# Staging slots at the start of the down-projection, an early query block, and the end of the attention written into the activation tile: one encoder kernel on one core

## The chip, the core and the metric

The kernel is one program on one NeuronCore of a Trainium2 chip. It runs a whole inference step of a two-layer encoder trunk. The metric is the device time in microseconds (us) from the launch to the end; lower is better. TensorE (PE) multiplies matrices, VectorE (DVE), ScalarE (ACT) and GpSimd (POOL) work element by element, and SyncE (SP) issues nearly all of the DMA transfers.

## The reference, cut to what matters

One prompt of 1024 tokens and eight samples of 16 tokens (128 tokens together) go through the same weights; the width is D = 1024, with 16 heads of 64. Layer 0 attends in a sliding window, layer 1 in a band of chunks over keys and values that are projected once, after layer 0.

```
for l in range(2):
    sh_m, sc_m, g_m, sh_f, sc_f, g_f = split(silu(c) @ w_ada[l] + b_ada[l], 6)
    h = x * (1 + sc_m) + sh_m
    o = band_attend(q(h), k, v, ...)          # l == 0: own k, v; l == 1: the shared k_b, v_b
    x = layer_norm(ALPHA * x + (1 + g_m) * (o @ w_o), ln_g[l, 0], ln_b[l, 0])
    h = x * (1 + sc_f) + sh_f
    u = h @ w_up[l]                           # 1024 -> 2 * 2816
    y = conv_b + sum(conv_w[tap] * u[t - 2 + tap] for tap in range(3))
    a, g = split(y, 2)
    x = layer_norm(ALPHA * x + (1 + g_f) * ((gelu(g) * a) @ w_down[l]), ln_g[l, 1], ln_b[l, 1])
    if l == 0:
        k_b, v_b = split((x * (1 + sc_kv) + sh_kv) @ w_kv_b)
```

Everything is float32. The samples attend also to cached keys and values, and the step returns the new keys, values and convolution rows beside the two outputs.

## The kernel before, in words

**Tiles and products.** The tokens are nine tiles of 128: tiles 0 to 7 are the prompt, tile 8 is the samples. Every operand of a large product is split in two: ACT casts the float32 value to a rounded high part (`copy`, line 161 in the profile), and POOL or DVE subtracts that from the value for the low part (`split`, line 172). A product is then three matmuls (low by high, high by low, high by high). `wload` (line 176 issues the DMA) loads a 128x1024 weight into a staging slot from the ring `self.ws`, and splits it into a pair of weight slots (hi, lo) from the ring `self.wring`. A ring hands out its buffers in turn; a load into a buffer waits until what was read from it before has been read.

**Order.** The program is written stage by stage, and a tile scheduler orders each engine's instructions by a simulated clock and by the dependences. On the chip SP, ACT, DVE and POOL each take their own instructions strictly in that order: an instruction that waits holds up all that stands behind it on its engine.

**Attention.** `qload(c)` and `qblock(c, bi)` load and compute the queries of head pair c (eight pairs; three blocks of 384 tokens each, the matmuls of line 291). The loop over `work` has 64 steps i; each issues scores (lines 544 and 547), softmax sums, transposes of the probabilities (lines 572 and 579), and the product with the values (line 594). Tables say at which step something else is issued: `QAT` the next query blocks, `ITEMS` the 16 sample items (eight samples by two halves p of the heads), `OAT` the reload of the finished outputs. A finished half of head pair c below 7 is normalised on POOL, written to a DRAM scratch `oN`, read back by `oload(c)` and split into the activation tile H. Pair 7 is split into H directly. The sample items go through the DRAM scratch `oSD` (eight 128x128 chunks).

**Output projection.** `out_proj` loads eight half-weights `wo` (its line numbers 967 on), then goes through the tiles in the order 8, 0, 1, ... 7: tile 8 first reads `oSD` and splits it; each tile takes two halves of 24 matmuls of 512 columns (`mmX`, line 304), and is then gated, added to the residual and normalised.

**Up- and down-projection.** The up-projection (line 1196) computes 22 blocks j of 128 channels; the convolution's taps (line 1035) and the product of gate and value run on DVE and POOL, and each block's result `act` is written to DRAM (`actD`, line 1083). The down-projection goes through the tiles in three groups of three, (0,1,2), (6,7,8), (3,4,5). In each group `fetch(j)` loads the weight j (`wdn`) by `wload`, reads the three tiles' part of `actD[j]` (line 1258), casts it on ACT and subtracts on DVE (line 1260), and 18 matmuls of 512 columns use it (line 1267). The staging ring for the weights is five slots in layer 0 and four in layer 1:

```
self.ws = Ring(narrow.items + [F[:, 0:1024]] + ([self.hf] if l else [self.lng, self.lnb]))
acts = Ring([... for i in range(12)])        # 12 pairs of 128x384 in X1
```

`narrow` is the two usual slots ws0 and ws1. `lng`, `lnb` are F[10368:12416], which overlaps F[10492:11644], the convolution's last row `y`; `hf` is F[4224:5248], which overlaps F[3876:5046], the last of the up-projection's buffers for u. In the third group the last 4 (layer 0) or 6 (layer 1) of the 22 weights and acts are kept, so that each tile of the group can be ended by itself. During group 0, after j = 8, `ln_gates` (lines 856 and 857) loads the gates and, in layer 1, `ln_rows` loads the rows of the last normalisation.

Of the kernel before, what the change touches and what calls it, by code (L numbers as in the profile page):

```python
# [10 lines left out]
F32 = mybir.dt.float32  # L11
# [27 lines left out]
QAT = {}  # L39
# [5 lines left out]
OAT = {51: (0, 1), 52: (2,), 53: (3,), 54: (4,), 55: (5,), 61: (6,)}  # L45
# [6 lines left out]
class Ring:  # L52
    def __init__(self, items):
        self.items = items
        self.i = 0

    def next(self):
        r = self.items[self.i % len(self.items)]
        self.i += 1
        return r  # L60
# [37 lines left out]
class Trunk:  # L98
    def __init__(self, ctx, tc, I, O):
# [39 lines left out]
        self.oSD = dr.tile([8, 128, 128], F32, name="oSD")  # L139
# [61 lines left out]
    def ada(self, gi, bank, ring=None):  # L201
# [36 lines left out]
        yield  # L238
# [132 lines left out]
    def attention(self, l, wk):  # L371
# [351 lines left out]
        def item_out(x):  # L723
            p, s = x.p, x.s
            t2 = self.bank(tbk.next())
            nc.tensor.transpose(t2[:, 0:128], osm, self.ident)
            if l == 0:
                if s == 0:
                    self.so = ost.next().rearrange("p (j t) -> p j t", t=128)
                so = self.so[:, :, 16 * s : 16 * s + 16]  # L730
            else:
                so = ost.next().rearrange("p (j q) -> p j q", q=16)
            for a in range(2):
                r = slice(64 * a, 64 * a + 64)
# [36 lines left out]
        for bi in range(3):  # L771
            qblock(0, bi, qw[0])
        items = [item(p, s) for p in range(2) for s in range(8)]
        steps = []
        for i, x in enumerate(work):
# [20 lines left out]
            for c in OAT.get(i, ()):  # L796
                oload(c)
        assert not items
# [167 lines left out]
    def out_proj(self, l, xsrc, xdst, aff):  # L966
        nc, I, H = self.nc, self.I, self.H
        wo = I[("wo0", "wo1")[l]]
# [4 lines left out]
        w = [self.wload(wo[i // 4, i % 4], el="ppppvvvv"[i], dst=d) for i, d in enumerate(loc)]  # L973
# [8 lines left out]
        for t in (8, 0, 1, 2, 3, 4, 5, 6, 7):  # L982
            c0 = t * 128
            if t == 8:
                s3 = self.xring.next().rearrange("p (c t) -> p c t", t=128)
                nc.sync.dma_start(s3, self.oSD.rearrange("c p t -> p c t"))
                self.split(s3, H[:, 0, :, c0 : c0 + 128], H[:, 1, :, c0 : c0 + 128], "a", "v")
            x = self.residual(t, xsrc)
            gate = self.gateP if t < 8 else self.gateS
            for hf in range(2):  # L990
                ps = self.bank(mb.next())
                self.mmX(ps, c0, (w0, w1)[hf], 2, 512)
                cs = slice(hf * 512, hf * 512 + 512)
                nc.vector.tensor_mul(self.tmp[:, cs], ps, gate[:, cs])
            nc.vector.scalar_tensor_tensor(x, x, ALPHA, self.tmp, op0=ALU.mult, op1=ALU.add)
            self.norm_tail(t, x, xdst, aff, False, tb, "a", "pv", Ring([self.xr]), hfr, hdst=self.hD)
# [236 lines left out]
    def down(self, l, xsrc, xdst, affs):  # L1233
# [8 lines left out]
        self.ws = Ring(narrow.items + [F[:, 0:1024]] + ([self.hf] if l else [self.lng, self.lnb]))  # L1242
        acts = Ring([(self.X1[:, i * 768 : i * 768 + 384], self.X1[:, i * 768 + 384 : i * 768 + 768]) for i in range(12)])
        ws = self.wslots
        order = [ws[2], ws[3], ws[0], ws[1]]
# [17 lines left out]
        def mm(j, w, a, gi, i):  # L1263
            for hf in range(2):
                ps = self.bank(GB[gi][2 * i + hf])
                for c, (p, q) in enumerate(((1, 0), (0, 1), (0, 0))):
                    nc.tensor.matmul(  # L1267
# [5 lines left out]
                    )  # L1273
# [33 lines left out]
        for gi, g in enumerate(GR):  # L1307
            keep = KEEP[l] if gi == 2 else 0
            for j in range(NFF - keep):
# [308 lines left out]
```

## Time and profile before

| | |
|---|---|
| median of 3 runs | 2878.46 us (2873.03 to 2889.01) |
| the profiled execution's own time | 2869.84 us |
| its span | 2868.1 us |
| mean granted PE clock | 0.979 |
| PE busy | 2719.9 us (95%) |
| DVE, ACT, POOL busy | 63%, 45%, 40% |
| DMA moved | 471.15 MB, mean 164 GB/s |

The stages of the span, by the first and last matmuls of each: opening to 58 us; layer 0's attention to about 380, its output projection to 495, up-projection to 1040, down-projection to 1353; the shared keys and values to 1565; layer 1's attention to 1959, its output projection to 2073, up-projection to 2565, down-projection to 2854. In the rows of the profile a line as "wh<-F" names what is written and what is read (F, X, H, C are the large tiles; wh, wl, xa pairs of hi and lo parts; ws the narrow staging slots). A figure in brackets behind a row is the idle time just before it on its engine, with what ended it.

### The profile page before, as it was taken

To read this page: it belongs to the slowest core of one execution; us is meant where nothing else is said; L and a number is where in the kernel's file an instruction comes from. 1 tells how busy PE (TensorE), PEld (TensorE's weight loads), DVE (VectorE), ACT (ScalarE), POOL (GpSimd) and SP (SyncE) were. 2 spreads that over 40 slices of the span, in tenths; PEclk is the share of its full clock that TensorE was granted. 3 is DMA by queue.
4 is the path that set the end of the run, shared out by engine and by line. 5 is a ranking of instruction groups with operands and counts; after the bars stand their busy time and mean duration, and the time that the engine had idled before them with its cause. 6 is when DMAs were issued, how large, how long until landed. Compare 5 with 4: busy or idle time off the path is not lost.

```text
span 2868.1 us, 47357 instructions
## 1 busy us (share of the span) xinstructions
PE 2719.9 (95%) x17734; PEld 2419.9 (84%) x17734; DVE 1820.3 (63%) x3674; ACT 1293.0 (45%) x2613; POOL 1157.0 (40%) x761
## 2 busy tenths in 40 slices
PE   7999899999999979999998999879999999999997
PEld 5888678889999968887998888757899999997886
DVE  4477777776667763564113667666797788883763
ACT  3476634433334333543225666652454444453442
POOL 2122424444434446655820122232454433447662
PEclk8999899999999989999999999989999999999999
DMA  8655454553444355664875357674432222246552
GB/s 297 213 166 168 135 171 167 188 191 137 142 157 140 124 174 184 228 218 155 287 239 178 108 154 198 166 216 141 167 122 85 70 80 70 70 147 235 206 197 79
DMA packets 221302, 471.15 MB, mean 164 GB/s; under 512 B 39856, under 2 KB 115840, under 8 KB 221072
## 3 DMA queue, kind: packets, MB, share of 16 engines
q1 hardware_dynamic: 221072, 468.13, 50.0%
q8 instruction: 139, 2.28, 0.3%
q14 instruction: 91, 0.75, 0.1%
HBM read 366.74 MB, written 110.74 MB: 166 GB/s over the span
## 4 chain that ended last, share of the span: by engine, by line
PE 79%; DMA 8%; DVE 5%; issue 2%; POOL 2%; ACT 2%; SPq 1%; POOLq 0%; DVEq 0%; ACTq 0%
PE PS L1196 30%; PE PS L1267 18%; PE PS L291 11%; PE PS L304 9%; PE PS L594 2%; PE PS L572 2%; PE PS L218 2%; PE PS L544 1%; PE PS L547 1%; DMA F<-in_wdn_dram 1%; PE PS L920 1%; DVE F L511 1%; POOL H L172 1%; PE PS L713 1%; DMA kH<-X 1%
## 5 line engine op out<-in xcount | busy, mean ns | idle before, releaser
L1196 PE MATMUL PS<-H,wh 128*128 128x256 f32 (+1 forms) x2560 | 395.2, 297 | 0.0
L1196 PEld LDWEIGHTS PS<-H,wh 128*128 128x128 f32 x2560 | 361.3, 191 | 0.4 <-issue 0.4
L1260 DVE TENSOR_TENSOR xa<-xa 128x384 fp32r<-128x384 f32 x132 | 186.7, 1426 | 226.1 <-ACT xa L161 223.9
L172 POOL TENSOR_TENSOR wl<-ws,wh 128x1024 fp32r<-128x1024 f32 x78 | 194.3, 2496 | 300.9 <-ACT wh L161 287.3
L161 ACT CAST wh<-F 128x512 fp32r<-128x512 f32 (+1 forms) x238 | 163.8, 693 | 326.1 <-PE PS L1196 153.1
L1267 PE MATMUL PS<-wh,xa 128*128 128x512 f32 x864 | 277.5, 397 | 25.1 <-ACT wh L161 25.1
L1158 DVE TENSOR_TENSOR F<-PS,F 128x192 f32<-128x192 f32 (+2 forms) x600 | 192.1, 350 | 167.8 <-PE PS L1196 164.9
L291 PE MATMUL PS<-H,wh 128*128 128x384 f32 (+1 forms) x1536 | 294.4, 337 | 0.0
L291 PEld LDWEIGHTS PS<-H,wh 128*128 128x128 f32 x1536 | 266.9, 188 | 1.4 <-issue 1.0
L1035 DVE SCALAR_TENSOR_TENSOR F<-F 128x1024 f32<-128x1024 f32 x320 | 257.6, 845 | 5.8 <-ACT F L1074 4.6
L1196 PE MATMUL PS<-H,wl 128*128 128x256 f32 (+1 forms) x1280 | 229.2, 299 | 9.7 <-ACT F L1163 5.5
L161 ACT CAST wh<-ws 128x1024 fp32r<-128x1024 f32 (+1 forms) x164 | 135.9, 834 | 221.8 <-PE PS L1196 92.2
L172 DVE TENSOR_TENSOR wl<-F,wh 128x512 fp32r<-128x512 f32 x198 | 200.9, 1022 | 37.7 <-ACT wh L161 37.7
L1267 PEld LDWEIGHTS PS<-wh,xa 128*128 128x128 f32 x864 | 163.9, 190 | 66.2 <-ACT wh L161 26.0
L1196 PEld LDWEIGHTS PS<-H,wl 128*128 128x128 f32 x1280 | 189.7, 190 | 17.4 <-ACT F L1163 5.9
L1196 PE MATMUL PS<-xa,wh 128*128 128x256 f32 (+1 forms) x1280 | 196.1, 295 | 0.6 <-DVE xa L172 0.6
L304 PE MATMUL PS<-wh,H 128*128 128x256 f32 (+1 forms) x936 | 172.0, 313 | 8.7 <-DVE H L172 5.3
L1196 PEld LDWEIGHTS PS<-xa,wh 128*128 128x128 f32 x1280 | 178.6, 188 | 1.4 <-DVE xa L172 1.0
L1044 POOL TENSOR_TENSOR F<-F 128x16 f32<-128x16 f32 x88 | 45.3, 515 | 331.0 <-DVE F L1035 247.1
L1267 PE MATMUL PS<-wl,xa 128*128 128x512 f32 x432 | 173.1, 401 | 0.2 <-POOL wl L172 0.2
L1267 PE MATMUL PS<-H,xa 128*128 128x512 f32 x684 | 161.3, 395 | 0.8 <-POOL H L172 0.8
L291 PE MATMUL PS<-H,wl 128*128 128x384 f32 (+1 forms) x768 | 155.3, 342 | 3.6 <-ACT H L161 2.5
(250 smaller groups left out, 5837.1 us busy)
## 6 DMA issues: line engine op xcount, KB each, us to landing
F<-in_wdn_dram SPq DMA_DIRECT2D x71, 512.0 KB
ws<-in_adaw_dram SPq DMA_DIRECT2D x64, 512.0 KB
ws<-in_wdn_dram SPq DMA_DIRECT2D x61, 512.0 KB
actD<-F SPq DMA_DIRECT2D x44, 576.0 KB
xa<-actD SPq DMA_DIRECT2D x132, 192.0 KB
ws<-in_wup_dram SPq DMA_DIRECT2D x49, 512.0 KB
F<-in_adaw_dram SPq DMA_DIRECT2D x48, 512.0 KB
F<-in_wup_dram SPq DMA_DIRECT2D x39, 512.0 KB
```

Of the source, the lines that this page charges most:

```text
L161: nc.scalar.copy(out, in_)
L172: self.eng(el).tensor_sub(lo, src, hi.bitcast(F32))
L218: mm = nc.tensor.matmul(ps[32 * j : 32 * j + 32, hf * 256 : hf * 256 + 256], self.cT[:, k * 32 : k * 32 + 32], w[:, j * 256 : j * 256 + 25 ...
L291: mm = self.nc.tensor.matmul(out[:, 0:n], w[a][:, k * 128 : k * 128 + 128], H[:, p, k, s0 : s0 + n], start=i == 0, stop=i == 23)
L304: self.nc.tensor.matmul(out[:, 0:n], H[:, p, j * kn + k, t0 : t0 + 128], w[a][:, k * n : k * n + n], start=i == 0, stop=i == 23,)
L572: nc.tensor.transpose(t[:, n * 128 : n * 128 + 128], p[:, (kt - k0) * 128 : (kt - k0) * 128 + 128], self.ident)
L594: mm = nc.tensor.matmul(ob[:, i0 * 128 : (i0 + n) * 128], vst[a][:, kt, :], pp[:, m * 128 : (m + n) * 128], start=cnt == 0, stop=cnt == to ...
L1035: nc.vector.scalar_tensor_tensor(o, u, cw[:, cc, i : i + 1], o, op0=ALU.mult, op1=ALU.add)
L1158: nc.vector.tensor_add(d, o, x)
L1196: self.pairmm = nc.tensor.matmul(ps[:, 0:m], w[a][:, k * 128 : k * 128 + 128], x(p, k, n), start=start and c == 0, stop=c == 11, skip_grou ...
L1260: nc.vector.tensor_sub(lo, raw, hi.bitcast(F32))
L1267: nc.tensor.matmul(ps, a[p][:, i * 128 : i * 128 + 128], w[q][:, hf * 512 : hf * 512 + 512], start=j == 0 and c == 0, stop=j == NFF - 1 an ...
```

## The change

It has four parts.

- **Down-projection.** A ring can have a list `first` that it hands out once before it goes round. In both layers the first five weights go to ws0, ws1, F[0:1024], F[11644:12668] and F[8700:9724] (the wide staging slots of the up-projection); the ring after that is as before, with `lng`, `lnb` or `hf`. The ring of acts has 6 pairs instead of 12, and the space X1[4608:8704] becomes two more pairs of weight slots (`order`: 6 to 8 in layer 0, 10 to 12 in layer 1). The loads of gates and rows after j = 8 are tied to the matmuls of that step (`issue_after`).
- **Early query block.** In layer 1, `qload(1)` and `qblock(1, 0)` come before the loop instead of at its steps 0 and 1.
- **End of the attention.** Head pair 6, as pair 7 before, is split straight into H, without the write to and read from `oN`. The sample items of the second half (p = 1, chunks 4 to 7) are split straight into H, per item in layer 1 and once in layer 0; `oSD` keeps four chunks, which `sload` reads at step 56. Four of the eight `wo` weights are loaded at the steps 57 to 60 of the loop (`woload`). `out_proj` computes the first halves of tiles 8 and 0 before their second halves.
- **Modulation.** One `yield` in `ada` is gone: a background row takes 17 steps in place of 18, which moves the loads of `adaw` and what follows them.

```
-OAT = {51: (0, 1), 52: (2,), 53: (3,), 54: (4,), 55: (5,), 61: (6,)}
+OAT = {51: (0, 1), 52: (2,), 53: (3,), 54: (4,), 55: (5,)}
+SAT = 56
+WAT = {57: 0, 58: 1, 59: 3, 60: 2}
 class Ring:
-    def __init__(self, items):
+    def __init__(self, items, first=()):
         self.items = items
+        self.first = list(first)
     def next(self):
+        if self.first:
+            return self.first.pop(0)
...
         nc.vector.tensor_add(row[:, 0:512], ps, row[:, 512:1024])
-        yield
...
-            if c < 7:
+            if c < 6:
                 nc.sync.dma_start(self.oN[c, r, q], on[r, q])
             elif a:
-                self.split(on[:, q], self.H[:, 0, 7, q], self.H[:, 1, 7, q], "a", "v")
+                self.split(on[:, q], self.H[:, 0, c, q], self.H[:, 1, c, q], "a", "v" if c == 7 else "p")
+        def sload():
+            s = self.ws.next()[:, 0:512].rearrange("p (c t) -> p c t", t=128)
+            nc.sync.dma_start(s, self.oSD.rearrange("c p t -> p c t"))
+            self.split(s, self.H[:, 0, 0:4, 1024:1152], self.H[:, 1, 0:4, 1024:1152], "a", "p")
...
-            oS = self.oSD[4 * p : 4 * p + 4].rearrange("c p t -> p c t")
-            if l:
-                nc.sync.dma_start(oS[:, :, 16 * s : 16 * s + 16], so)
-            elif s == 7:
-                nc.sync.dma_start(oS, self.so)
+            if p == 0:
+                ... (as before, into oSD)
+            elif l or s == 7:
+                src = so if l else self.so
+                c0 = 1024 + 16 * s if l else 1024
+                hs = [self.H[:, i, 4:8, c0 : c0 + (16 if l else 128)] for i in range(2)]
+                self.split(src, *hs, "a", "p" if l else "v")
...
             qblock(0, bi, qw[0])
+        if l:
+            qload(1)
+            qblock(1, 0, qw[1])
...
-            for c, bi in QAT.get(i, ()):
+            for c, bi in QAT.get(i, ()) if l == 0 or i > 1 else ():
...
+            if i == SAT:
+                sload()
+            if i in WAT:
+                self.woload(l, WAT[i])
...
-        w = [self.wload(wo[i // 4, i % 4], el="ppppvvvv"[i], dst=d) for i, d in enumerate(loc)]
+        w = [self.wo[i] if i in self.wo else self.woload(l, i) for i in range(8)]
...
-            if t == 8:
-                s3 = self.xring.next().rearrange("p (c t) -> p c t", t=128)
-                nc.sync.dma_start(s3, self.oSD.rearrange("c p t -> p c t"))
-                self.split(s3, H[:, 0, :, c0 : c0 + 128], H[:, 1, :, c0 : c0 + 128], "a", "v")
+        for t in order[:2]:
+            half(t, 0)
+        for t in order:
+            if t not in order[:2]:
+                half(t, 0)
+            half(t, 1)
...
-        self.ws = Ring(narrow.items + [F[:, 0:1024]] + ([self.hf] if l else [self.lng, self.lnb]))
-        acts = Ring([... for i in range(12)])
+        slots = narrow.items + [F[:, 0:1024]]
+        self.ws = Ring(slots + ([self.hf] if l else [self.lng, self.lnb]), slots + [F[:, 11644:12668], F[:, 8700:9724]])
+        acts = Ring([... for i in range(6)])
-        order = [ws[2], ws[3], ws[0], ws[1]]
+        order = [ws[2], ws[3], ws[0], ws[1]] + [tuple(self.X1[:, o + 1024 * a : o + 1024 * a + 1024] for a in range(2)) for o in (4608, 6656)]
...
                 if gi == 0 and j == 8:
-                    self.ln_gates(l, 1)
-                    if l:
-                        self.ln_rows(l, 1)
+                    with self.tc.issue_after(self.downmm):
+                        self.ln_gates(l, 1)
+                        if l:
+                            self.ln_rows(l, 1)
```

What the change does to the order of instructions is seen at three places. The first is SP's queue around layer 0's last write of `actD`, where the down-projection starts (`in_wdn_dram` is a weight, `xa<-actD` an act, `F<-gd` the gates). Before:

```order
L176 DMA ws<-in_wdn_dram 128x1024
L1050 DMA out_conv_dram<-F 128x198
L1258 DMA xa<-actD 128x384 x2
L176 DMA ws<-in_wdn_dram 128x1024
L1083 DMA actD<-F 128x1152
L856 DMA F<-gd 128x1024
L857 DMA F<-gd 128x1x1024
L1258 DMA xa<-actD 128x384
L176 DMA F<-in_wdn_dram 128x1024 x4
L1258 DMA xa<-actD 128x384
L176 DMA F<-in_wdn_dram 128x1024
L1258 DMA xa<-actD 128x384
```

After:

```order
L181 DMA ws<-in_wdn_dram 128x1024
L1081 DMA out_conv_dram<-F 128x198
L1290 DMA xa<-actD 128x384
L181 DMA F<-in_wdn_dram 128x1024
L1290 DMA xa<-actD 128x384
L1114 DMA actD<-F 128x1152
L879 DMA F<-gd 128x1024
L880 DMA F<-gd 128x1x1024
L1290 DMA xa<-actD 128x384
L181 DMA F<-in_wdn_dram 128x1024 x2
L1290 DMA xa<-actD 128x384
```

The last write of `actD` stood behind eight loads of down weights, and the loads into F behind it; now eleven are ahead of it, and two loads into F follow it after the gates and one act.

The second place is PE at the start of layer 1's attention loop (line 291, in the changed kernel 295, is the query block; 544 and 547, now 548 and 551, are the scores; 304, now 308, a projection ahead of it). Before:

```order
L304 MATMUL PS<-wl,H 128x256 x4
L304 MATMUL PS<-wh,H 128x256 x4
L291 MATMUL PS<-H,wh 128x384 x14
L291 MATMUL PS<-H,wl 128x384 x8
L291 MATMUL PS<-H,wh 128x384 x16
L544 MATMUL PS<-xa 128x128
L547 MATMUL PS<-xa 128x128
L544 MATMUL PS<-xa 128x256
L547 MATMUL PS<-xa 128x256
```

After:

```order
L308 MATMUL PS<-wh,H 128x256 x4
L295 MATMUL PS<-H,wh 128x384 x14
L295 MATMUL PS<-H,wl 128x384 x8
L295 MATMUL PS<-H,wh 128x384 x16
L295 MATMUL PS<-H,wl 128x384 x8
L295 MATMUL PS<-H,wh 128x384 x16
L548 MATMUL PS<-xa 128x128
L551 MATMUL PS<-xa 128x128
L548 MATMUL PS<-xa 128x320
L551 MATMUL PS<-xa 128x320
```

One more group of 24 query matmuls (8 with the low weight, 16 with the high one) stands ahead of the first scores; it stood after them.

The third place is PE at the end of layer 1's attention (line 594, now 598, is the product with the values; 572, now 576, the transposes; 713, now 722, and 726, now 735, the samples' product and its transposition; `H 128x512` of line 304, now 308, are matmuls of the output projection). Before:

```order
L572 MATMUL PS<-C,F 128x128 x4
L726 MATMUL PS<-C 128x128
L572 MATMUL PS<-C,F 128x128 x4
L304 MATMUL PS<-xa,H 128x512 x5
L572 MATMUL PS<-C,F 128x128 x8
L594 MATMUL PS<-wh,xa 128x512 x2
L594 MATMUL PS<-wl,xa 128x512 x2
L572 MATMUL PS<-C,F 128x128 x4
L594 MATMUL PS<-wh,xa 128x384 x2
L594 MATMUL PS<-wh,xa 128x128 x2
L594 MATMUL PS<-X_70,xa 128x384 x2
L594 MATMUL PS<-X_70,xa 128x128 x2
L304 MATMUL PS<-wh,H 128x512 x2
```

After:

```order
L576 MATMUL PS<-C,F 128x128 x4
L722 MATMUL PS<-F,C 32x128 x12
L308 MATMUL PS<-xa,H 128x512 x5
L576 MATMUL PS<-C,F 128x128 x4
L735 MATMUL PS<-C 128x128
L576 MATMUL PS<-C,F 128x128 x4
L308 MATMUL PS<-xa,H 128x512 x12
L576 MATMUL PS<-C,F 128x128 x4
L598 MATMUL PS<-wh,xa 128x512 x2
L598 MATMUL PS<-wl,xa 128x512 x2
L576 MATMUL PS<-C,F 128x128 x4
L598 MATMUL PS<-wh,xa 128x384 x2
```

Of the output projection's matmuls, 5 lie here between the transposes before, and 17 now; up to the last product with the values there are 62 of them in this stretch before, and 84 now (31 and 67 in layer 0).

More of the change, by code (lines that the diff above doesn't have):

```diff
@@ L138, in __init__ @@
         self.oN = dr.tile([7, 128, 1024], F32, name="oN")
-        self.oSD = dr.tile([8, 128, 128], F32, name="oSD")
+        self.oSD = dr.tile([4, 128, 128], F32, name="oSD")
         self.rD = [dr.tile([16, 1024], F32, name=f"rD{l}") for l in range(2)]
@@ L735, in item_out @@
                 nc.vector.tensor_copy(so[r], t2[r, 0:128].rearrange("p (j a q) -> p j a q", j=4, a=2)[:, :, a, :])
-            oS = self.oSD[4 * p : 4 * p + 4].rearrange("c p t -> p c t")
-            if l:
-                nc.sync.dma_start(oS[:, :, 16 * s : 16 * s + 16], so)
-            elif s == 7:
-                nc.sync.dma_start(oS, self.so)
+            if p == 0:
+                oS = self.oSD.rearrange("c p t -> p c t")
+                if l:
+                    nc.sync.dma_start(oS[:, :, 16 * s : 16 * s + 16], so)
+                elif s == 7:
+                    nc.sync.dma_start(oS, self.so)
+            elif l or s == 7:
[3 more added lines that the diff above has]
+                self.split(src, *hs, "a", "p" if l else "v")
         def item(p, s):
@@ L772, in attention @@
             qblock(0, bi, qw[0])
+        if l:
+            qload(1)
+            qblock(1, 0, qw[1])
         items = [item(p, s) for p in range(2) for s in range(8)]
+        self.wo = {}
         steps = []
@@ L963, in residual, with woload @@
         return x
-    def out_proj(self, l, xsrc, xdst, aff):
-        nc, I, H = self.nc, self.I, self.H
-        wo = I[("wo0", "wo1")[l]]
+    def woload(self, l, i):
         X1, X2 = self.X1, self.X2
@@ L972, in out_proj @@
         loc = self.wslots[0:2] + loc + [self.wslots[2], (X1[:, 4096:5120], X2[:, 0:1024])]
-        w = [self.wload(wo[i // 4, i % 4], el="ppppvvvv"[i], dst=d) for i, d in enumerate(loc)]
+        self.wo[i] = self.wload(self.I[("wo0", "wo1")[l]][i // 4, i % 4], el="ppppvvvv"[i], dst=loc[i])
+        return self.wo[i]
+    def out_proj(self, l, xsrc, xdst, aff):
+        nc, I, H = self.nc, self.I, self.H
+        w = [self.wo[i] if i in self.wo else self.woload(l, i) for i in range(8)]
         w0, w1 = w[0:4], w[4:8]
@@ L981, in out_proj, with half @@
         hfr = Ring([self.hf, self.zt])
-        for t in (8, 0, 1, 2, 3, 4, 5, 6, 7):
-            c0 = t * 128
-            if t == 8:
-                s3 = self.xring.next().rearrange("p (c t) -> p c t", t=128)
-                nc.sync.dma_start(s3, self.oSD.rearrange("c p t -> p c t"))
-                self.split(s3, H[:, 0, :, c0 : c0 + 128], H[:, 1, :, c0 : c0 + 128], "a", "v")
+        order = (8, 0, 1, 2, 3, 4, 5, 6, 7)
+        acc = {}
+        def half(t, hf):
+            acc[t, hf] = self.bank(mb.next())
+            self.mmX(acc[t, hf], t * 128, (w0, w1)[hf], 2, 512)
+        for t in order[:2]:
[4 more added lines that the diff above has]
+            half(t, 1)
             x = self.residual(t, xsrc)
@@ L990, in out_proj @@
             for hf in range(2):
-                ps = self.bank(mb.next())
-                self.mmX(ps, c0, (w0, w1)[hf], 2, 512)
                 cs = slice(hf * 512, hf * 512 + 512)
-                nc.vector.tensor_mul(self.tmp[:, cs], ps, gate[:, cs])
+                nc.vector.tensor_mul(self.tmp[:, cs], acc[t, hf], gate[:, cs])
             nc.vector.scalar_tensor_tensor(x, x, ALPHA, self.tmp, op0=ALU.mult, op1=ALU.add)
@@ L1241, in down @@
         narrow = self.ws
-        self.ws = Ring(narrow.items + [F[:, 0:1024]] + ([self.hf] if l else [self.lng, self.lnb]))
-        acts = Ring([(self.X1[:, i * 768 : i * 768 + 384], self.X1[:, i * 768 + 384 : i * 768 + 768]) for i in range(12)])
+        slots = narrow.items + [F[:, 0:1024]]
+        self.ws = Ring(slots + ([self.hf] if l else [self.lng, self.lnb]), slots + [F[:, 11644:12668], F[:, 8700:9724]])
+        acts = Ring([(self.X1[:, i * 768 : i * 768 + 384], self.X1[:, i * 768 + 384 : i * 768 + 768]) for i in range(6)])
         ws = self.wslots
-        order = [ws[2], ws[3], ws[0], ws[1]]
+        order = [ws[2], ws[3], ws[0], ws[1]] + [tuple(self.X1[:, o + 1024 * a : o + 1024 * a + 1024] for a in range(2)) for o in (4608, 6656)]
         if l == 0:
@@ L1266, in mm @@
                 for c, (p, q) in enumerate(((1, 0), (0, 1), (0, 0))):
-                    nc.tensor.matmul(
+                    self.downmm = nc.tensor.matmul(
                         ps,
@@ L1272, in mm @@
                         stop=j == NFF - 1 and c == 2,
-                    )
+                    ).ins
         def evict(t, gi, i):
@@ L1313, in down @@
                 if gi == 0 and j == 8:
-                    self.ln_gates(l, 1)
-                    if l:
-                        self.ln_rows(l, 1)
+                    with self.tc.issue_after(self.downmm):
+                        self.ln_gates(l, 1)
+                        if l:
+                            self.ln_rows(l, 1)
             if gi == 0:
```

## The prediction

> **What bounds the kernel now.** I read the page first: the span, PE's share, and the chain that ended last by engine.
>
> ```profile
> span 2868.1 us, 47357 instructions
> PE 2719.9 (95%) x17734; PEld 2419.9 (84%) x17734; DVE 1820.3 (63%) x3674; ACT 1293.0 (45%) x2613; POOL 1157.0 (40%) x761
> PE 79%; DMA 8%; DVE 5%; issue 2%; POOL 2%; ACT 2%; SPq 1%; POOLq 0%; DVEq 0%; ACTq 0%
> ```
>
> PE is the bound: it is busy for 2719.9 of 2868.1 us, so 148 us of its idle time is all that better order can bring without fewer matmuls, and the change removes no matmul. The next view is busy time by stretch (columns: stretch, length, then PE, PEld, DVE, ACT and POOL busy, granted PE clock, DMA share, GB/s), around the places that the change touches.
>
> ```profile
> 360.00:385.00 25.00, 18.00 (x109) 12.74 (x108) 16.77 (x30) 11.09 (x18) 9.30 (x8) 0.93 0.64 207
> 1040.00:1076.00 36.00, 18.04 (x76) 14.24 (x75) 15.44 (x19) 10.27 (x14) 16.58 (x8) 0.76 0.60 171
> 1076.00:1350.00 274.00, 273.33 (x1225) 221.65 (x1223) 133.81 (x191) 113.65 (x168) 164.49 (x69) 1.00 0.56 191
> 1560.00:1580.00 20.00, 10.82 (x51) 10.03 (x51) 11.66 (x30) 14.76 (x31) 0.00 (x0) 0.83 0.59 164
> 1855.00:1970.00 115.00, 88.01 (x630) 64.03 (x627) 63.46 (x192) 56.38 (x119) 32.49 (x23) 0.88 0.70 204
> ```
>
> The body of the down-projection (third row) has no idle time to give. PE idles for 18.0 us at layer 0's down start, 9.2 at layer 1's loop start, 27.0 at the end of layer 1's attention and 7.0 at the end of layer 0's. The edits act there, so I price each place by its own rows. The sum is made against the profiled execution's own time, 2869.84 us; the median of the runs, 2878.46, is 8.6 above it, and I add that at the end.
>
> **Layer 0, start of the down-projection.** PE's timeline, two DMAs of the chain, the clock, and the taps of the convolution on DVE in layer 0 and in layer 1:
>
> ```profile
> 1040.59 0.39 PE L1267 MATMUL PS<-wh,xa 128*128 128x512 f32 x1
> ...
> 1052.96 0.39 PE L1267 MATMUL PS<-wh,xa 128*128 128x512 f32 x1
> 1071.31 2.93 PE L1267 MATMUL PS<-wh,xa 128*128 128x512 f32 x6 [17.96 <-ACT wh L161]
> ...
> 1076.89 8.56 PE L1267 MATMUL PS<-X,xa 128*128 128x512 f32 x36
> ```
>
> ```profile
> 1055.27 3.36 DMA actD<-F
> 1058.69 11.45 DMA F<-in_wdn_dram
> ```
>
> ```profile
> 1071.00:1074.00 3.00, 2.69 (x6) 2.06 (x7) 0.00 (x0) 1.30 (x2) 2.67 (x2) 0.50 0.00 0
> ```
>
> ```profile
> 1045.47 4.41 DVE L1035 SCALAR_TENSOR_TENSOR F<-F 128x1024 f32<-128x1024 f32 x6
> ...
> 2571.70 8.72 DVE L1035 SCALAR_TENSOR_TENSOR F<-F 128x1024 f32<-128x1024 f32 x6
> ```
>
> From 1040.59 to 1052.96 are 54 matmuls, three weights, at 0.233 us each, so a weight lasts 4.2 us. Weight j = 3 is the first in `lng`, whose load waits until the last `actD` write, issued at 1055.27, has read `y`; the load takes 11.45 us, and PE has nothing for 17.96. It then runs 18 matmuls from 1071.31 to 1076.89, 5.58 us in place of 4.2, at a granted clock of 0.50: 1.4 more. The price of the gap is 19.3. With `first`, j = 3 and 4 get slots that are free, and j = 5 to 7 come from the narrow slots, as the order shows; the first weight behind the write is now j = 8, in `lng`. PE reaches it at 1040.6 + 8 × 4.2 = 1074, just after the 1071 at which a weight in `lng` was usable before. The write may come later: its taps took 4.41 us in layer 0, and 8.72 in layer 1 where POOL splits weights beside them, which it now does here too. 4.3 us later is 1075.6, plus up to 9 us where two loads share the DMA queues as the four did (about 11.45 us each). The rest is 0 to 10; I take 4, nearest to the taps' difference, and a gain of 15 (9 to 19).
>
> The Trainium skill, page "SBUF — State Buffer", section "Who interferes with whom", says that a DVE instruction with two SBUF inputs and a GpSimd instruction that reads SBUF lock each other out. By it moving POOL's splits to the taps has this price; the 4.41 against 8.72 us agree.
>
> **Layer 1, start of the down-projection.**
>
> ```profile
> 2565.16 0.39 PE L1267 MATMUL PS<-wh,xa 128*128 128x512 f32 x1
> ...
> 2585.09 2.93 PE L1267 MATMUL PS<-wh,xa 128*128 128x512 f32 x6 [7.17 <-ACT wh L161]
> ...
> 2591.78 13.00 PE L1267 MATMUL PS<-H,xa 128*128 128x512 f32 x55
> ```
>
> The idle 7.17, and 6.69 in place of 4.2 us for the next 18 matmuls (2585.09 to 2591.78), are 9.7 us. Weight j = 3 is the one in `hf`, which overlaps the last u; after the change j = 3 and 4 have free slots, and `hf` is first needed for j = 8, at 2565.2 + 8 × 4.2 = 2599, 14 us after the 2585 at which it was usable before. Gates and rows load beside it, which gives back 0 to 5, I take 1: gain 8.5 (5 to 10).
>
> **Layer 1, loop start.**
>
> ```profile
> 1563.58 1.66 PE L291 MATMUL PS<-H,wl 128*128 128x384 f32 x8 [2.54 <-ACT H L161]
> 1565.08 2.94 PE L291 MATMUL PS<-H,wh 128*128 128x384 f32 x16
> ...
> 1574.52 0.58 PE L544 MATMUL PS<-xa 128*128 128x256 f32 x1 [6.33 <-DVE xa L498]
> ```
>
> PE waits 6.33 us for DVE's queries. The 24 moved matmuls last 1.50 + 2.8 = 4.3 us (starts 1563.58 and 1565.08, and 2.94 less the overlap) and fall into it, and a remaining gap of 2 us should leave more of the clock, which I put at 0.7: 5 (0 if the block's weights are late, 6.5 at most).
>
> **Layer 1, end of the attention.** PE, then ACT's queue, the two DMAs of the samples and the clock:
>
> ```profile
> 1891.81 1.66 PE L713 MATMUL PS<-F,C 128*32 128x128 f32 x24 [4.42 <-DMA F<-in_cvB_dram]
> ...
> 1919.28 1.11 PE L572 MATMUL PS<-C,F 128*128 128x128 f32 x4 [5.35 <-DVE X L579]
> ...
> 1959.27 1.22 PE L304 MATMUL PS<-wh,H 128*128 128x512 f32 x2 [3.58 <-DVE H L172]
> ```
>
> ```profile
> 1916.33 1.04 ACT L161 CAST H<-ws 128x1024 fp32r<-128x1024 f32 x1 [5.08 <-DMA ws<-oN]
> ...
> 1956.91 1.04 ACT L161 CAST H<-F 128x1024 fp32r<-128x1024 f32 x1 [4.34 <-DMA F<-oSD]
> ```
>
> ```profile
> 1948.58 3.63 DMA oSD<-F
> 1952.23 4.66 DMA F<-oSD
> ```
>
> ```profile
> 1919.00:1924.00 5.00, 4.72 (x19) 4.19 (x19) 3.22 (x8) 1.17 (x2) 0.86 (x1) 0.50 0.42 134
> 1959.00:1965.00 6.00, 5.73 (x14) 4.49 (x15) 0.82 (x2) 0.00 (x0) 0.00 (x0) 0.50 1.02 284
> ```
>
> ACT's cast of pair 6 waits 5.08 us for the read of `oN` and holds up the casts of probabilities behind it, so PE idles 5.35. Without `oN` this wait is gone. The samples' write (3.63) and read (4.66) and the cast end at 1957.95, DVE's subtraction follows, and PE idles 3.58; now only a small split follows the last item. The two windows at half clock, 4.72 and 5.73 busy, cost half of that, at most 2.4 and 2.9; the later one has its DMAs at 1.02, and I count 1.7 and 2.6. Sum 5.35 + 3.58 + 1.7 + 2.6 = 13.2. On the other side stand new in-order waits on ACT: the casts of `sload` and of four `wo` weights. Two of these weight loads now stand ahead of a load of cached values, which already costs 4.42. I take 10 (3 to 13).
>
> **Layer 0, end of the attention.**
>
> ```profile
> 372.28 1.04 ACT L161 CAST xa<-ws 128x1024 fp32r<-128x1024 f32 x1 [6.32 <-DMA ws<-in_wo_dram]
> ```
>
> ```profile
> 379.81 0.73 PE L304 MATMUL PS<-wh,H 128*128 128x512 f32 x2 [1.74 <-DVE H L172]
> ```
>
> ```profile
> 380.00:384.00 4.00, 4.00 (x13) 3.16 (x13) 3.91 (x5) 2.22 (x4) 0.57 (x1) 0.65 0.85 259
> ```
>
> The 7.0 us idle of this stretch lie before output-projection matmuls and the last products; ACT waits 6.32 for a `wo` weight, which is now loaded in the loop, and 67 output matmuls stand ready in place of 31 (36 × 0.233 = 8.4 us of cover). With 1.4 for the clock (4 us at 0.65) the price is 8.4; I take 6 (0 to 8).
>
> The Trainium skill, page "TensorE: Matmul & The Clock Gate", Part 1, says that the clock halves after an idle window of about 3.4 us and returns after as long a busy one. By it the gap of 1.74 here costs no clock and the sum is 1.4 less. The granted 0.50 behind the four gaps above agrees, the 0.65 here does not.
>
> **What costs nothing, and its cover.** Six pairs of acts in place of twelve: layer 1's third group and a change of groups show what an act needs.
>
> ```profile
> 2739.53 0.32 SPq L1258 DMA_DIRECT2D xa<-actD  x1
> ```
>
> ```profile
> 2742.46 1.53 DVE L1260 TENSOR_TENSOR xa<-xa 128x384 fp32r<-128x384 f32 x1 [2.67 <-ACT xa L161]
> ```
>
> ```profile
> 2782.26 0.45 SPq L1258 DMA_DIRECT2D xa<-actD  x1
> ```
>
> ```profile
> 2799.81 0.52 ACT L161 CAST xa<-xa 128x384 fp32r<-128x384 f32 x1 [9.27 <-DMA xa<-actD]
> ```
>
> From issue (2739.53) to use (2743.99) are 4.5 us, and five pairs ahead cover 5 × 4.2 = 21. At a change of groups SP stands behind other work from 2782.26 until acts come again (cast at 2799.81): 17.6 us, still under 21. Without this cover each of the four changes of groups (two per layer) would cost what exceeds it. The gates tied to j = 8 stand where they stood, nothing. The missing `yield` shifts the loads of `adaw` by a step; they are read in stretches where PE has no idle row for them: 0, with −4 to +4, about half the idle time at layer 0's end on either side, since the scheduler puts the rows around them in another order too. The two extra weight pairs only ease waits.
>
> **The sum.** 15 + 8.5 + 5 + 10 + 6 = 44.5; 2869.84 − 44.5 = 2825, and plus 8.6 on the median's footing 2834. With all low ends (9, 5, 0, 3, 0 and −4) it is 2865, with all high ends (19, 10, 6.5, 13, 8, 4) 2818; not all go one way, so the own range is 2819 to 2847. 0.5% is 14.4 us, about what a measurement can tell from no change, from 2864.1 to 2892.9.
>
> **The rivals.**
> - *The attention ends stay as long.* ACT waits in `sload` or a `wo` cast as it did for `oN` (5.08) and `wo` (6.32). For it speaks that ACT's order is strict and those loads are put among the last casts; against it that they are issued many steps ahead. The last two terms fall away: 2834 + 16 = 2850. Chance 0.16.
> - *The gap at layer 0's down start reopens at j = 8.* For it: the load in `lng` still stands behind the last write, and POOL slows the taps. The term is about 7 in place of 15: 2842. Chance 0.12.
> - *Net nothing.* Six acts do not cover the changes of groups, four times about 5 us, and the ends of the attention stall: 2834 + 20 + 16 = 2870 (2865 to 2878). Chance 0.08.
> - *Slower, by the acts.* The block at a change of groups decides from 21 us on. Before, it lasted 17.6 with twelve pairs ahead; if it grew by 18 us or so because the acts of the next group can't be fetched early, the loss is 15 at each of four places, 60 less 44.5: about 2893. Chance 0.04, since the cover holds by 3 us in the rows.
>
> **The chances.** The forecast, 2834, has 0.60. Faster by over 0.5% is the forecast and the first two rivals, 0.88, less 0.01 for their edge: 0.87; within 0.5% the third, 0.09 with that edge; slower 0.04. The range, from 2815 (high ends, less noise of 3) to 2858 (the first rival with low ends in the down starts), leaves out about 2 in 10.
>
> **What the changed profile would show.** Right: no idle PE row over 5 us in the first 15 us of either down-projection, a granted clock of 1.00 there; the first scores of layer 1 after less than 3 us of idle time; no ACT cast from `oN` for pair 6; the output projection's tile 8 without a wait for a DVE split. Wrong: an idle gap released by the cast of `wh` or by an act eight weights into layer 0's down-projection; a cast from `ws` with 5 us before it at the attention's end; PE waiting for `xa` at a change of groups in the down-projections.

## The result and the profile after

The changed kernel takes 2827.48 us (median of 4 runs, 2823.97 to 2830.02) against 2878.28 us: ratio 0.9826, 95% interval 0.9804 to 0.9847, or 44 to 56 us less. The forecast was 2834, with a range from 2815 to 2858. The profiled execution of the changed kernel took 2830.02 us, the slowest of its four, and that of the kernel before 2869.84, faster than any run beside it; the two spans therefore differ by only 39.9 us.

The first lines of the page: span and busy time.

```profile
span 2828.2 us, 47410 instructions
PE 2717.7 (96%) x17734; PEld 2419.7 (86%) x17734; DVE 1813.6 (64%) x3673; ACT 1294.3 (46%) x2624; POOL 1171.1 (41%) x773
```

PE does the same 17734 matmuls in 2.2 us less of busy time, so of the 39.9 us between the spans 37.7 are idle time. Busy time by stretch (same columns as before), for the stretches that answer to those of the kernel before: the end of layer 0's attention, both down starts, the body of layer 0's down-projection, layer 1's loop start and attention end.

```profile
362.00:393.00 31.00, 27.83 (x178) 20.68 (x177) 15.36 (x44) 11.72 (x23) 10.57 (x8) 0.97 0.41 139
...
1048.00:1083.00 35.00, 35.00 (x153) 28.32 (x152) 18.94 (x15) 11.71 (x15) 21.62 (x10) 1.00 0.67 202
1083.00:1329.00 246.00, 246.00 (x1086) 199.57 (x1085) 129.91 (x184) 105.10 (x158) 155.33 (x64) 1.00 0.60 206
...
1548.00:1565.00 17.00, 12.55 (x67) 11.30 (x68) 12.57 (x31) 12.89 (x25) 0.00 (x0) 1.00 0.48 133
...
1834.00:1940.00 106.00, 86.38 (x650) 63.08 (x649) 61.73 (x192) 58.31 (x129) 35.26 (x31) 0.94 0.65 196
...
2536.00:2577.00 41.00, 41.00 (x180) 33.25 (x179) 20.48 (x15) 16.67 (x22) 31.35 (x14) 1.00 0.80 249
```

Both down starts are full at a granted clock of 1.00 (18.0 and 8.1 us were idle). Layer 1's loop start idles 4.5 us in place of 9.2, its attention end 19.6 in place of 27.0, and layer 0's attention end 3.2 in place of 7.0.

For the comparison of all kernels below I cut each trace at PE's first matmul of a stage, by its timeline, and give the stretches that the change touches, in us. "Attention 0" runs from layer 0's first scores to its up-projection; "KV and attention 1" from the end of layer 0's down-projection to layer 1's up-projection.

| kernel | attention 0 | down 0 | KV and attention 1 | down 1 |
|---|---|---|---|---|
| before | 429.1 | 302.1 | 768.8 | 288.2 |
| changed | 432.3 | 281.2 | 752.8 | 277.2 |
| down part alone | 434.6 | 281.4 | 756.4 | 276.3 |
| query block alone | 431.0 | 304.7 | 760.6 | 288.4 |
| attention end alone | 435.7 | 303.4 | 759.7 | 289.0 |
| one yield less alone | 439.8 | 303.3 | 766.5 | 288.5 |
| end in layer 1 alone | 431.3 | 304.4 | 763.2 | 287.9 |
| end in layer 0, yield | 429.3 | 304.4 | 764.1 | 288.1 |

One trace is one execution. The same down-projection differs by 0.9 us or less between kernels that have the whole part, by up to 2.6 between those that don't; the attention, which waits for DMAs, differs by 5 us and more without an edit in it. So the sizes of the parts are taken from the timed ratios, and the traces say where, as far as they do: attention 0 is 3.2 us longer in the changed trace than before, though its end idles less.

### The profile page after: what moved, and what is told of

Read it like the earlier page. It is cut to its first block, busy times and chain, and to the rows that moved or that the text cites. A ratio compares the mean times of both kernels' runs of the same rounds, so it can differ in the third digit from the quotient of the medians.

```text
span 2828.2 us, 47410 instructions
## 1 busy us (share of the span) xinstructions
PE 2717.7 (96%) x17734; PEld 2419.7 (86%) x17734; DVE 1813.6 (64%) x3673; ACT 1294.3 (46%) x2624; POOL 1171.1 (41%) x773
## 5 line engine op out<-in xcount | busy, mean ns | idle before, releaser
L177 POOL TENSOR_TENSOR wl<-ws,wh 128x1024 fp32r<-128x1024 f32 x72 | 182.1, 2533 | 276.9 <-ACT wh L166 263.9
L166 ACT CAST wh<-F 128x512 fp32r<-128x512 f32 (+1 forms) x230 | 155.1, 681 | 296.2 <-PE PS L1227 150.5
L1066 DVE SCALAR_TENSOR_TENSOR F<-F 128x1024 f32<-128x1024 f32 x320 | 265.7, 871 | 4.8 <-ACT F L1105 3.4
L166 ACT CAST wh<-ws 128x512 fp32r<-128x512 f32 (+1 forms) x158 | 129.6, 825 | 207.7 <-PE PS L1227 89.7
L1299 PE MATMUL PS<-wh,xa 128*128 128x512 f32 x696 | 222.5, 396 | 0.0
L1299 PEld LDWEIGHTS PS<-wh,xa 128*128 128x128 f32 x696 | 130.6, 188 | 30.6
L166 ACT CAST xa<-xa 128x384 fp32r<-128x384 f32 x132 | 67.5, 513 | 186.5 <-DMA xa<-actD 186.4
L636 POOL TENSOR_TENSOR F<-F,X 64x512 f32<-64x512 f32 x62 | 80.3, 1295 | 171.1 <-DVE F L612 134.1
```

Of the source, the lines that this page charges most:

```text
L166: nc.scalar.copy(out, in_)
L177: self.eng(el).tensor_sub(lo, src, hi.bitcast(F32))
L1066: nc.vector.scalar_tensor_tensor(o, u, cw[:, cc, i : i + 1], o, op0=ALU.mult, op1=ALU.add)
L1299: self.downmm = nc.tensor.matmul(ps, a[p][:, i * 128 : i * 128 + 128], w[q][:, hf * 512 : hf * 512 + 512], start=j == 0 and c == 0, stop=j ...
```

## The experiments

**One part at a time.** Each kernel is the kernel before with one part of the change.

Down part alone:

```
-        self.ws = Ring(narrow.items + [F[:, 0:1024]] + ([self.hf] if l else [self.lng, self.lnb]))
+        self.ws = Ring(slots + ([self.hf] if l else [self.lng, self.lnb]), slots + [F[:, 11644:12668], F[:, 8700:9724]])
+        (six acts, two more weight pairs, gates behind the matmuls of j = 8)
```

> The kernel before with the down-projection's part alone (slots, six acts, two more weight pairs, the gates' place). Theory: the part is worth what the two starts lost before, gap and slow clock together, since the changed trace shows no idle time at either start (0.00 us in the first 35 and 41 us): 19.3 + 10 = 29 to 32 us faster, ratio 0.989, PE idle under 1 us in both starts, and the same times elsewhere. Rival (the forecast's terms): a residual wait at j = 8 stays in layer 0 and the gates cost in layer 1, 15 + 8.5 = 23.5, ratio 0.992.

Measured: ratio 0.9877 (0.9855 to 0.9899), 35 us less (29 to 42). The two starts, by stretch:

```profile
1043.00:1079.00 36.00, 35.14 (x173) 29.41 (x172) 18.99 (x23) 11.43 (x14) 22.39 (x10) 1.00 0.72 211
2535.00:2576.00 41.00, 39.85 (x194) 33.30 (x193) 25.01 (x25) 17.98 (x22) 35.28 (x15) 1.00 0.73 230
```

Both clocks are 1.00, and the idle time left in these stretches (0.86 and 1.15) lies in the up-projection's last matmuls, since no idle time lies behind the first matmul of either down-projection. The measured 35 fits the theory, and the forecast's 23.5 is below the interval.

Query block alone:

```
+        if l:
+            qload(1)
+            qblock(1, 0, qw[1])
...
-            for c, bi in QAT.get(i, ()):
+            for c, bi in QAT.get(i, ()) if l == 0 or i > 1 else ():
```

> The kernel before with the early query block alone. Theory: 24 matmuls of about 4.3 us fall into the 6.33 us of idle time ahead of the second scores: 4 to 6 us faster, ratio 0.998, idle under 2.5 us there, granted clock of that stretch near 1.00. Rival: the loop behind it has its own limit (ACT and DVE) and gives the time back: 0 to 1 us.

Measured: 0.9983 (0.9971 to 0.9994), 4.9 us (1.7 to 8.3). PE goes into the scores with 0.70 and 0.66 us of idle time:

```profile
1576.94 2.94 PE L291 MATMUL PS<-H,wh 128*128 128x384 f32 x16
1580.57 0.33 PE L544 MATMUL PS<-xa 128*128 128x128 f32 x1 [0.70 <-DVE xa L498]
...
1581.68 0.41 PE L544 MATMUL PS<-xa 128*128 128x320 f32 x1 [0.66 <-DVE xa L498]
```

One yield less alone:

```
         nc.vector.tensor_add(row[:, 0:512], ps, row[:, 512:1024])
-        yield
```

> The kernel before with one yield less in the modulation rows alone. Theory A: it moves the loads of the modulation's weights so that PE waits for them in layer 0's attention (2.29 and 2.05 us in the changed trace, with a slower clock of 0.93 between 202 and 302 us): 4 to 8 us slower, ratio 1.002, all of it before 540 us and in the up-projection of layer 0. Theory B: it moves work that is hidden: within 2 us.

Measured: 1.002 (1.0006 to 1.0034), 5.8 us slower (1.7 to 9.8). Attention 0 has 439.8 us in its trace against 429.1. PE waits for a weight of the modulation, and later for an output weight's cast:

```profile
254.23 0.87 PE L218 MATMUL PS<-ws,C 128*32 128x256 f32 x8 [2.04 <-DMA ws<-in_adaw_dram]
...
385.10 3.34 PE L303 MATMUL PS<-xa,H 128*128 128x512 f32 x6 [2.77 <-ACT xa L161]
```

The first of these waits stands between 251 and 255 us, with 1.8 to 2.4 us, in the trace of every kernel without the yield, and in none with eighteen steps. The size and the stage fit theory A; the up-projection, which it also named, was only 1.5 us longer.

Attention end alone, in both layers (the diff of that part, without the yield). An output weight takes the modulation row's staging slot between its sum and its use here, so the second row of layer 0 holds other values than the reference's; the instructions are the same in number and shape. By the code this is why the yield has to go with the loads in the loop.

> The kernel before with the attention's end alone (pair 6 and the second half of the samples straight into the activation tile, four output weights in the loop, first halves of two tiles first), in both layers; the yield stays. Theory A: layer 1 gains 9 to 10, and layer 0, where the changed trace was 4.8 us later at the end of the output projection, gains 4 to 6 without the yield's loss: 13 to 16 us faster, ratio 0.995. Theory B: the attention's end itself makes layer 0 longer by about 5 (67 output matmuls stand ahead of the last products with the values in place of 31): 4 to 6 us faster in all, ratio 0.998.

Measured: 0.9962 (0.9949 to 0.9974), 10.9 us (7.5 to 14.7): above theory B, and in the interval only the low values of theory A. So the layers were taken apart.

```
+END = (1,)
...
+            if c < (6 if l in END else 7):
...
+            if i in WAT and l in END:
```

> The kernel before with the attention's end in layer 1 alone. Theory A (the forecast's term): the waits for pair 6 (5.35 us) and for the samples' round trip (3.58 us) and their slow clock go: 9 to 11 us faster, ratio 0.9965. Theory B: the wait of 5.35 us belongs to some executions only, since it was 1.71 us in two kernels whose attention end is as before: 4 to 7 us faster, ratio 0.998.

Measured: 0.9972 (0.9961 to 0.9983), 8.1 us (4.9 to 11.2). It doesn't decide between A and B, whose values both lie in the interval.

```
+END = (0,)
...
-        yield
```

> The kernel before with the attention's end in layer 0 alone, and one yield less in the modulation rows. Theory A: the two add, layer 0's end gives 0 to 2 and the yield costs 5.8 as it did alone: 4 to 6 us slower, ratio 1.0015. Theory B: they do not add, the row that ends three steps earlier makes room for the output weights in the loop: 0 to 4 us faster, ratio 0.999.

Measured: 0.9977 (0.9965 to 0.9989), 6.6 us faster (3.2 to 10.1). Theory A is out: the yield costs 5.8 us alone, and not with layer 0's end. In its trace attention 0 takes 429.3 us, as before (429.1), and the 4.7 us less stand in KV and attention 1, where it has no edit; so where the 6.6 us lie is not shown.

**The number of steps in the changed kernel.**

```
+        yield
         row = ring.next()
```

> The changed kernel with eighteen steps to a modulation row again: the yield stands before the row's buffer is taken instead of behind the sum. Theory A: the missing step costs in the changed kernel what it cost alone, so this one is 4 to 6 us faster than the changed kernel, ratio to the kernel before 0.981. Theory B: with the output weights in the loop the later end of the rows costs as much: 0.9826 as the changed kernel, or up to 0.984.

Measured: 0.983 (0.9809 to 0.9851), as the changed kernel; attention 0 takes 431.4 us against 432.3, though the wait of 2.05 us near 254 is gone. This fits theory B; theory A's 0.981 lies at the edge of the interval and is not excluded. No loss from the eighteenth step is measured, if it stands before the row takes its slot.

**The margin at j = 8.** In the changed trace the last six taps, the last write of acts and the two loads into `lng` and `lnb` behind it, the casts, the subtraction for j = 8, and the first matmul that reads it:

```profile
1051.23 8.78 DVE L1066 SCALAR_TENSOR_TENSOR F<-F 128x1024 f32<-128x1024 f32 x6
```

```profile
1063.06 0.32 SPq L1114 DMA_DIRECT2D actD<-F  x1
...
1066.34 0.95 SPq L181 DMA_DIRECT2D F<-in_wdn_dram  x2
```

```profile
1076.32 2.22 ACT L166 CAST wh<-F 128x1024 fp32r<-128x1024 f32 x2
```

```profile
1078.87 2.43 POOL L177 TENSOR_TENSOR wl<-F,wh 128x1024 fp32r<-128x1024 f32 x1
```

```profile
1081.62 0.39 PE L1299 MATMUL PS<-wl,xa 128*128 128x512 f32 x1
```

The taps took 8.78 us beside POOL's splits, as the forecast had it from layer 1's 8.72. The down-projection began at 1047.98, and PE came to j = 8 after 33.4 us, at 1081.39. POOL's subtraction is over at 1081.30, and PE first reads it at 1081.62. The gap was closed with 0.3 us to spare. In the other traces with the whole part it is from 0.8 us to none: with the casts on POOL, below, PE waits 0.16 us there.

```
-        self.ws = Ring(..., slots + [F[:, 11644:12668], F[:, 8700:9724]])
+        self.ws = Ring(..., slots + [F[:, 11644:12668]])
```

> The changed kernel with four slots in the list that is handed out first, so that the weight in the slot behind the last write of the acts is j = 7 in place of j = 8. Theory: in the changed trace that weight was usable 33.4 us after the start of layer 0's down-projection, and PE came to j = 8 at 33.6, so there was no margin: for j = 7 PE comes at 29.4 and idles 3 to 5 us, with 1 to 2 us of slow clock behind it, and layer 1 stays without a gap: 4 to 6 us slower than the changed kernel, ratio to the kernel before 0.984. Rival: the weight is not bound to that write, no idle row over 1 us there, 0.9826.

Measured: 0.9846 (0.9826 to 0.9866), 44.3 us less than before in place of 50.1; the two intervals overlap, and it is the trace that shows the gap. PE idles at j = 7, 31.4 us after its start, and the clock falls:

```profile
1077.56 2.87 PE L1299 MATMUL PS<-X,xa 128*128 128x512 f32 x7 [1.80 <-POOL X L177]
```

```profile
1077.00:1082.00 5.00, 4.44 (x12) 3.50 (x13) 3.58 (x2) 1.25 (x2) 3.16 (x2) 0.66 0.79 253
```

Down 0 takes 284.8 us, 3.6 more: 1.8 idle and 1.7 by the clock (5 us at 0.66). The gap is there, smaller than expected, because the write was issued earlier in this kernel (1059.00, 12.9 us after the start against 15.1).

**Acts and weight pairs.**

```
-        acts = Ring([... for i in range(6)])
+        acts = Ring([... for i in range(12)])
-        order = [...] + [two pairs in X1]
+        order = [...]
```

> The changed kernel with twelve pairs of acts and without the two extra pairs of weight slots, as before, so that the down-projection's part is the list of first slots and the gates' place alone. Theory: six acts and the extra weight pairs are worth nothing, the slots are all: down-projections of 281 and 277 us as in the changed kernel, ratio to the kernel before 0.9826. Rival: the extra weight pairs let the first weights be split ahead, and without them a gap of 2 us or more stands in the first 40 us of a down-projection: 0.984 or more.

Measured: 0.9873 (0.986 to 0.9887), 36.6 us, so 13.5 us of the gain are gone. The theory that the slots are all falls: a gap stands at j = 8.

```profile
1082.80 0.50 PE L1299 MATMUL PS<-wh,xa 128*128 128x512 f32 x1 [1.23 <-ACT wh L166]
...
1085.41 0.50 PE L1299 MATMUL PS<-wl,xa 128*128 128x512 f32 x1 [2.11 <-POOL wl L177]
```

```profile
1066.82 0.32 SPq L1114 DMA_DIRECT2D actD<-F  x1
```

The last write is issued 19.0 us after the start (1047.81) in place of 15.1. Down 0 takes 288.0 us, 6.8 more. The last kernel has six acts without the extra pairs:

> The changed kernel with six acts but without the two extra pairs of weight slots. With twelve acts and without the extra pairs the last write of the acts was issued 19.0 us after the start of layer 0's down-projection, against 15.1 in the changed kernel, and PE idled 3.34 us at j = 8. Theory: the extra pairs are the cause, since with them fewer splits wait on POOL among the last pieces of the convolution; six acts change nothing: again a gap of 2 to 5 us at j = 8, layer 0's down-projection of 285 to 289 us, ratio to the kernel before 0.987. Rival: the number of acts is the cause, by the order in which SP issues them: no gap, 281 us, 0.9826.

Measured: 0.9825 (0.9811 to 0.9839), as the changed kernel. Its trace has 1.12 us of idle time in down 0 (the larger piece below) and 284.3 us in all, 3.1 more than the changed kernel's.

```profile
1088.11 0.50 PE L1299 MATMUL PS<-wl,xa 128*128 128x512 f32 x1 [0.89 <-POOL wl L177]
```

Neither theory holds whole: the ratio speaks for the number of acts, the trace for a small part of the extra pairs. The write was issued 15.8 us after the start there (1064.29 against 1048.53). In the three kernels that wait, with four first slots, with six acts only and with twelve, PE reads the subtracted weight 18.6, 18.5 and 18.6 us after the issue of that write: the time of the write decides.

Why twelve acts put it later is seen on DVE, here with twelve acts and then with six, both without the extra pairs:

```profile
1051.39 11.93 DVE L1066 SCALAR_TENSOR_TENSOR F<-F 128x1024 f32<-128x1024 f32 x8
```

```profile
1049.14 9.91 DVE L1066 SCALAR_TENSOR_TENSOR F<-F 128x1024 f32<-128x1024 f32 x8
```

With twelve acts, six of their subtractions (line 1292) stand on DVE between 1042.45 and 1051, ahead of the last eight taps, which end 15.5 us after the start; with six acts none does, and the taps end after 10.5. The extra pairs do something else too. In the changed trace the weights j = 4 and 5 lie in them (first row), j = 6 and 7 in slots that layer 0 had before (second row):

```profile
1064.78 8.36 PE L1299 MATMUL PS<-xa 128*128 128x512 f32 x36
1072.98 8.58 PE L1299 MATMUL PS<-X,xa 128*128 128x512 f32 x36
```

The same 36 matmuls take 0.2 us less from the extra pairs, each time these come round, without idle time on either side; the reason is not shown. From j = 4 to the last matmul layer 0's down-projection takes 264.0 us in the changed trace and 265.4 in the one before. So of the 3.1 us some 1.4 are this and the rest the small gaps. Of the 13.5 us with twelve acts 6.8 lie in down 0; 4.8 lie in KV and attention 1, which this edit does not touch and where six acts only has as much in its trace without a slower ratio. What is left of the 13.5 beside the 6.8 stays open.

**What holds ACT.**

```
-            self.split(s, self.H[:, 0, c, 0:1024], self.H[:, 1, c, 0:1024], "a", "p")
+            self.split(s, self.H[:, 0, c, 0:1024], self.H[:, 1, c, 0:1024], "p", "p")
```

> The changed kernel with the high parts of the pairs 0 to 5, which are reloaded from DRAM at the attention's end, made on POOL in place of ACT. Theory: the largest gap that is left there (5.40 us at 1844.5, behind an ACT cast that waits 3.18 us for such a reload while the casts of probabilities stand behind it) is the wait in ACT's strict order, the mechanism of the 5.35 us of pair 6; on POOL the wait holds up nothing that PE needs soon: the gap falls under 2 us and the kernel gains 4 to 8 us, ratio to the kernel before 0.980. Rival: POOL, with two passes over each pair in place of one, is late with the normalisation of the next pairs and with the samples' splits: a new gap of the same size or more, 0.9826 to 0.986.

The changed kernel, ACT and PE at the gap that was left:

```profile
1842.09 1.04 ACT L166 CAST H<-ws 128x1024 fp32r<-128x1024 f32 x1 [3.18 <-DMA ws<-oN]
```

```profile
1844.52 1.97 PE L576 MATMUL PS<-C,F 128*128 128x128 f32 x8 [5.40 <-DVE wh L583]
```

Measured: 0.9856 (0.9842 to 0.9869), 8.6 us slower than the changed kernel. The mechanism was right and the expectation wrong: no gap over 1 us is left where the 5.40 stood, but a wait for a DMA takes its place 20 us further on (305 us behind the first scores, against 286). Most of the loss lies elsewhere: layer 0's attention is 6.7 us longer in the trace (439.0), for a reason not followed up.

```profile
1869.27 0.89 PE L687 MATMUL PS<-F 128*32 128x272 f32 x8 [4.17 <-DMA F<-kS]
```

**The output weights.**

```
-WAT = {57: 0, 58: 1, 59: 3, 60: 2}
+WAT = {}
```

> The changed kernel with all eight output weights loaded after the loop in program order, as before. Theory: the loads in the loop are what fills PE ahead of the last products, since the first halves of tiles 8 and 0 need them: without them 3 to 5 us are lost at each end, ratio to the kernel before 0.985. Rival: the scheduler issues them as early anyway: 0.9826.

Measured: 0.9835 (0.9822 to 0.9849), 2.6 us slower than the changed kernel, which the intervals do not separate. In the traces attention 0 is 5.3 us longer, with the wait below, and KV and attention 1 differ by 0.6: if the loads in the loop bring anything, it lies in layer 0, and 5.3 us is no more than this stage differs by without an edit.

```profile
375.62 4.62 PE L308 MATMUL PS<-xa,H 128*128 128x512 f32 x9 [2.70 <-ACT xa L166]
```

No kernel tried was faster than the changed one by more than the intervals.

## Why the prediction was right, by its own steps

| term | forecast | measured |
|---|---|---|
| both down starts | 15 + 8.5 | 35 (29 to 42) |
| loop start | 5 (0 to 6.5) | 4.9 (1.7 to 8.3) |
| layer 1's end | 10 (3 to 13) | 8.1 (4.9 to 11.2) |
| layer 0's end, with the yield | 6 + 0 | 6.6 (3.2 to 10.1) |
| sum | 44.5 | 50 (44 to 56), the parts 55 |

The places and the waits were right, and the sum is in the range. The sizes were less so: the down starts' 35 lies above the forecast's own high ends (19 + 10), and the sum came within 6 us of the forecast also because the parts overlap. By stage, in the two traces, down 0 gives 20.9 us and down 1 11.0, loop start and layer 1's end together 16.0 (forecast 15), and attention 0 gives nothing (3.2 longer, forecast 6 shorter).

- **Layer 0's down start** was mis-sized, by its rest and by its price. The rest of 4 us at j = 8 was 0.00. The price of 19.3 came from one execution; the five other traces without the part idle 18.6 to 19.3 us there, and down 0 takes 304.0 on average in them against 281.2, so 22 to 23 us go, 1.4 of them by the shorter matmuls from the extra pairs, a term that the forecast did not have. The row that the forecast took for the rest, slower taps, was right (8.78 us); but the write came 15.1 us after the start against 14.7 before, since POOL's last product followed the taps at once (first fence, changed), where it had stood behind a split of POOL's, 2.4 us after their end at 1049.88 (second fence, before). That it came just in time for j = 8, by 0.3 us, is luck: the forecast expected to be 4 us late.

```profile
1060.18 2.85 POOL L1113 TENSOR_TENSOR F<-F 128x1152 f32<-128x1152 f32 x1 [0.33 <-DVE F L1066]
```

```profile
1049.92 2.42 POOL L172 TENSOR_TENSOR wl<-ws,wh 128x1024 fp32r<-128x1024 f32 x1
1052.29 2.95 POOL L1082 TENSOR_TENSOR F<-F 128x1152 f32<-128x1152 f32 x1
```

- **Layer 1's down start** gave 11 to 12 us (288.4 to 277) and not 8.5: of what the forecast gave back to the gates and rows, 1 us, only one idle time of 0.58 us is seen (at 2578.96, before an act).
- **The loop start** was right in size and cause; the first scores of the changed kernel come after idle times of 1.41 and 0.67 us.
- **Layer 1's end** was right in size. In the changed trace no cast of pair 6 from `oN` is left, and where 3.58 us of waiting for DVE stood, PE waits 1.74 for an ACT cast:

```profile
1939.68 1.20 PE L308 MATMUL PS<-xa,H 128*128 128x512 f32 x4 [1.74 <-ACT xa L166]
```

 But one of its two waits was not as fixed as the forecast had it. The 5.35 us behind pair 6's cast are 1.71 in the two kernels that only change something earlier:

```profile
1900.04 0.66 PE L575 MATMUL PS<-C,F 128*128 128x128 f32 x4 [1.71 <-DVE X L582]
```

```profile
1897.73 1.05 ACT L164 CAST H<-ws 128x1024 fp32r<-128x1024 f32 x1 [1.99 <-DMA ws<-oN]
```

 (PE and ACT, down part alone.) Their order has a cast of probabilities ahead of pair 6's cast on ACT, where the kernel before has it behind; an edit elsewhere changed the order that the scheduler chose. In the kernel with one yield less, whose order there is the old one, the wait is 5.05. So part of this gain belongs to whichever part of the change comes first, which may be one reason that the parts sum to more than the whole.
- **Layer 0's end** came out at 6.6 with the yield's effect, against 6 with 0. The forecast had the sum right and not its inside: the yield alone costs 5.8 us (1.7 to 9.8), where it had 0 and at most 4, and the two don't add. Since the traces do not show the gain in that stage, the agreement of 6 and 6.6 may be luck.
- **Six acts** were said to cost nothing, and there is no idle time at a change of groups (in layer 0, 246.00 of 246.00 us busy in the third row above; in layer 1 the 0.58 us is the only idle time of the down-projection). But they were worth more than nothing: with twelve acts and no extra pairs 13.5 us are lost. That the extra pairs "only ease waits" was wrong by the 1.4 us above.
- **The rivals.** The reopened gap at j = 8 did not come, with 0.3 us to spare, and comes with one slot less or with twelve acts. Slow attention ends did not come in layer 1, whose end idles 19.6 us in place of 27.0; in layer 0 the end idles less, but the whole attention is not shorter in the trace. The two rivals by the acts at the changes of groups are out, by the full third row.

## What to carry to other kernels

A wait that opens a stage is closed when the first weights get buffers that nothing late still reads; count how many weights it takes until the late buffer's turn, since here seven weights were too few and eight just enough, by 0.3 us. In a kernel whose order comes from a simulated clock, an edit moves waits in stages it does not touch, so time the parts apart and don't take the sum of one trace's gaps for the gain. A cast that waits for a DMA in the middle of ACT's queue costs what stands behind it, but before taking it away look at what waits next: here, once, it was another transfer.

## What the runs showed of the hardware

The clock can fall behind gaps that are short: 0.66 in the five us behind an idle time of 1.80 us, as the 0.65 behind 1.74 us in the kernel before. So a gap of 1.8 us cost 3.6 us of the stage. The Trainium skill, page "TensorE: Matmul & The Clock Gate", Part 1, has the clock fall after an idle window of about 3.4 us; these two rows differ, and the measurement decides. It does not always fall: at layer 1's loop start in the changed kernel idle times of 2.14 and 1.41 us leave it at 1.00; which gaps do it is not shown. The taps of the convolution took twice their time, 8.78 us for six against 4.41, as soon as POOL's splits were moved beside them; the write behind them came only 0.4 us later, because POOL's last product no longer stood behind one of these splits. The 36 matmuls of two weights took 8.36 us from one pair of buffers and 8.58 from another, at a clock of 1.00.
